# Latent attention in a two-layer trunk: the value product turned round, sums applied behind it, projections between the blocks

## Chip, cores and metric

The kernel runs on one core of one Trainium2 chip. The metric is the device time of the whole launch in microseconds; of the kernel before three runs are known, and their median is the figure that counts.

## What is computed

Two layers of a decoder trunk, 512 tokens of width 1024, float32. Each layer is FFN, token mixer, FFN; every part has a norm ahead and behind, and is scaled, shifted and gated by vectors that come from a conditioning input. Layer 0 mixes by latent attention, layer 1 by a dilated attention. What the change touches is the latent attention and the vectors:

```python
mod = (silu(c) @ w_mod[i] + b_mod[i]).reshape(B, N_SUB, 3, D_MODEL)
...
lat = h @ w_in
cq = lat[..., :Q_LORA]                      # 384
ckv = lat[..., Q_LORA:Q_LORA + KV_LORA]     # 256
k_rope = lat[..., Q_LORA + KV_LORA:]        # 32
q = (rmsnorm(cq, q_norm) @ w_q_up)          # 16 heads of 64 + 32
kv = (rmsnorm(ckv, kv_norm) @ w_kv_up)      # 16 heads of 64 + 64
...
s = einsum('bhqd,bhkd->bhqk', qi, kt) * scale      # causal, blocks of 128 queries
p = softmax(s, axis=-1)
o = einsum('bhqk,bhkd->bhqd', p, vt)
...
return o.reshape(B, S, MLA_HEADS * V_HEAD) @ w_o
```

## The kernel before

The activations lie transposed, 128 partitions by 8 tiles of 512 tokens. Every large product goes as three fp32r passes (`mm3`, L119 to L122): high by high, high by low, low by high. Weights come by DMA on SyncE's queue into a ring of five raw buffers (`load`, L92 to L96), are split into a high part on ScalarE (L103) and a low part on VectorE (L105, two halves), and lie in a ring of six.

The conditioning vectors are made 128 numbers at a time: `mod` loads 512 KB of `w_mod` and multiplies and sums them on VectorE (L128). The vectors that a later part needs wait in the list `todo`; `pump` takes one from it, and `settle` takes what is left for a part before that part needs it. In the first FFN `pump` is called after each head (a gate and up unit) and after each of the first 16 down units; in the attention, after each value product.

A list scheduler sets the order on each engine from the order in which the program is written and from priorities; the copy-out of a finished result has a high one (`HOT`).

The latent attention runs so. Its `head` units make six latents; `norm` scales them (L600, L603, L604), and one of them carries the shared rope key, made by L581 to L583. Then `rest`:

- `values` makes v for all 16 heads, 8 units of six passes, from two normalised latents.
- `keys(g)` makes keys, rope parts and queries of four heads; it is a generator, advanced one piece after every second block while the heads of the group ahead are worked on.
- `attend` takes one head's block of 128 queries: `score` (L671), the causal correction with the row minimum on VectorE (L673), the exponential with the row sum on ScalarE (L676); `turn` transposes the probabilities (L683) and copies them out (L686, L688); `weigh` multiplies them with v (L694), probabilities as the stationary block, and after the fourth block scales each row by the reciprocal of its sum (L703, L707); `close` transposes the result of two heads (L719) and `put_o` splits it into high and low (L550, L551). `Pipe(1)` sets how many steps lie between `score` and `turn`.
- `out_unit` then makes the first three of eight tiles of the output product.

```python
                nc.tensor.matmul(
                    box["o"][:, i * 64 : i * 64 + 64],
                    box[i][:, j * P : (j + 1) * P],
                    self.v[j, h // 8][:, (h % 8) * 64 : (h % 8) * 64 + 64],
```

Of the kernel before, what the change touches and what calls it, by code (L numbers as in the profile page):

```python
# [51 lines left out]
class Trunk:  # L52
    def __init__(self, ctx, tc, a):
        self.ctx, self.tc, self.nc, self.a = ctx, tc, tc.nc, a
        nc = tc.nc
        self.cp = ctx.enter_context(tc.tile_pool(name="const", bufs=1))
        self.ring = ctx.enter_context(tc.tile_pool(name="ring", bufs=SLOTS))
        self.sl = ctx.enter_context(tc.tile_pool(name="sl", bufs=SLICES))
        self.tmp = ctx.enter_context(tc.tile_pool(name="tmp", bufs=2))
        self.ps = ctx.enter_context(tc.tile_pool(name="ps", bufs=4, space=PSUM))  # L60
        self.chunks = {}
# [343 lines left out]
class Ffn:  # L405
# [76 lines left out]
    def rest(self):  # L482
        t = self.t
        for q, (at, n) in enumerate(GROUPS):
# [71 lines left out]
class Mla(Mixer):  # L556
# [53 lines left out]
            t.mm3(b, [x[:, at + j, :] for x in w], self.latn[u], j == 0, j == len(us) - 1)  # L610
        return b

    def values(self):
        t, nc = self.t, self.t.nc
        w = [t.weights(t.a["mla_v"][k], flat=True) for k in range(2)]
        self.v = {}
        for j in range(4):
            for e in range(2):
                b = t.bank()
                for k in range(2):  # L620
                    ls = [x[:, j * P : (j + 1) * P] for x in self.latn[k]]
                    t.mm3(b, ls, [x[:, e * SEQ : (e + 1) * SEQ] for x in w[k]], k == 0, k == 1)
                self.v[j, e] = t.s()
                t.pump(1)
                nc.scalar.activation(self.v[j, e], b, AF.Copy)

    def keys(self, g):
        t, nc = self.t, self.t.nc
        w = []
        q, k = [[t.s() for _ in range(4)] for _ in range(2)]  # L630
        self.qk[g] = q, k

        def pair(p, x, ci, at, us):
            if len(w) <= ci:
                w.append(t.weights(t.a[f"mla_qk{ci}"][g]))
            b = self.project(w[ci], at, us)
            nc.scalar.activation(x[2 * p][0:64], b[0:64], AF.Copy)
            nc.vector.tensor_copy(x[2 * p + 1][0:64], b[64:128])
            if x is k:
                for y in k[2 * p : 2 * p + 2]:  # L640
                    nc.gpsimd.tensor_scalar(y[64:96], self.lat[2][64:96], 1.0, 0.0, ALU.mult, ALU.add)

        def rope():
            b = self.project(w[0], 4, (3, 4, 5))
            t1, t2 = t.t("u", UB), t.t("u", UB)
            nc.vector.stream_shuffle(t2, b, [(c + 16) % 32 for c in range(32)])
            nc.vector.tensor_tensor(t1, b, self.cos, ALU.mult)
            nc.gpsimd.tensor_tensor(t2, t2, self.sin, ALU.mult)
            for j in range(4):
                r = slice(32 * j, 32 * j + 32)  # L650
                nc.vector.tensor_tensor(q[j][64:96], t1[r], t2[r], ALU.add)

        yield pair(0, k, 0, 0, (0, 1))
        yield rope()
        yield pair(0, q, 1, 0, (3, 4, 5))
        yield pair(1, k, 0, 2, (0, 1))
        yield pair(1, q, 1, 3, (3, 4, 5))

    def attend(self, h, q, k, pipe, at):
        t, nc = self.t, self.t.nc  # L660
        sc = 96.0**-0.5
        if at == 0:
            self.st = t.tmp.tile([P, 8], F32, tag="st", name="st", bufs=3), {}
        st, box = self.st
        nm, z = st[:, 0:4], st[:, 4:8]

        def score(i):
            n = (i + 1) * P
            c = slice(i, i + 1)
            s = t.bank()[:, :n]  # L670
            nc.tensor.matmul(s, q[0:96, i * P : n], k[0:96, :n], start=True, stop=True)  # L671
            p = box[i] = t.t("sq", SB)[:, :n]
            nc.vector.tensor_tensor_reduce(  # L673
                p, s, self.mask[:, SEQ - n :], -sc, 3e38, ALU.add, ALU.min, accum_out=nm[:, c]
            )
            nc.scalar.activation(p, p, AF.Exp, bias=nm[:, c], scale=-1.0, accum_out=z[:, c])  # L676

        def turn(i):
            n = (i + 1) * P
            x = t.bank("aux")[:, :n]  # L680
            for j in range(i + 1):
                r = slice(j * P, (j + 1) * P)
                nc.tensor.transpose(x[:, r], box[i][:, r], t.ident)  # L683
            box[i] = t.t("silu" if i % 2 else "gg")[:, :n]
            if i == 3:
                nc.scalar.activation(box[i], x, AF.Copy)  # L686
            else:
                nc.vector.tensor_copy(box[i], x)  # L688

        def weigh(i):  # L690
            if i == 0:
                box["o"] = t.bank("aux")
            for j in range(i + 1):
                nc.tensor.matmul(  # L694
                    box["o"][:, i * 64 : i * 64 + 64],
                    box[i][:, j * P : (j + 1) * P],
                    self.v[j, h // 8][:, (h % 8) * 64 : (h % 8) * 64 + 64],
                    start=j == 0,
                    stop=j == i,
                )  # L700
            if i < 3:
                return
            nc.vector.reciprocal(z, z)  # L703
            if h % 2 == 0:
                self.os = t.t("acc")
            dst = self.os.rearrange("p (i e c) -> p i e c", i=4, e=2)[:, :, h % 2, :]
            nc.vector.tensor_tensor(  # L707
                dst,
                box["o"][:, :256].rearrange("p (i c) -> p i c", i=4),
                z.unsqueeze(2).to_broadcast([P, 4, 64]),  # L710
                ALU.mult,
            )

        def close(i):
            if i == 3 and h % 2:
                x = t.bank("aux")
                for j in range(4):
                    r = slice(j * P, (j + 1) * P)
                    nc.tensor.transpose(x[:, r], self.os[:, r], t.ident)  # L719
                self.put_o(x)  # L720

        pipe.push(at, score, turn, weigh, close)

    def rest(self):
        t = self.t
        self.values()
        self.qk = {}
        pipe = Pipe(1)
        for _ in self.keys(0):
            pass  # L730
        for g in range(4):
            ahead = self.keys(g + 1) if g < 3 else iter(())
            q, k = self.qk[g]
            for j in range(4):
                for i in range(4):
                    self.attend(4 * g + j, q[j], k[j], pipe, i)
                    if (4 * j + i) % KQ == KQ - 1:
                        next(ahead, None)
            for _ in ahead:
                pass  # L740
        pipe.flush()
        for k in range(KT - TAIL):
            self.out_unit(k, 0, SEQ)


class Dil(Mixer):
# [8 lines left out]

    def tables(self):
        t, nc = self.t, self.t.nc
        t.dram = t.ctx.enter_context(t.tc.tile_pool(name="dr", bufs=1, space=bass.MemoryType.DRAM))
# [439 lines left out]
```

## Time and profile before

| what | before |
|---|---|
| median of three runs | 2365.59 us (2364.16 to 2369.31) |
| profiled execution, its own time | 2368.39 us |
| its span, first to last instruction | 2366.2 us |
| mean granted TensorE clock | 0.989 |
| TensorE busy | 2295.6 us, 97% |
| VectorE busy | 1213.2 us, 51% |
| ScalarE busy | 841.8 us, 36% |
| GpSimd busy | 206.4 us, 9% |
| data moved by DMA | 281.5 MB, 119 GB/s on average |

The shares are means over the whole span; the attention is one stage of it, from the first value product at 454.70 us to the last output matmul ahead of the second FFN at 617.40 us. Busy time counts neither register nor DMA-issuing instructions. The matmuls overlap, so that their busy times are longer than the distance between two starts; the granted clock is a share of 2.4 GHz.

### The profile page before, as it was taken

To read this page: it belongs to the slowest core of one execution; us is meant where nothing else is said; L and a number is where in the kernel's file an instruction comes from. 1 tells how busy PE (TensorE), PEld (TensorE's weight loads), DVE (VectorE), ACT (ScalarE), POOL (GpSimd) and SP (SyncE) were. 2 spreads that over 40 slices of the span, in tenths; PEclk is the share of its full clock that TensorE was granted. 3 is DMA by queue.
4 is the path that set the end of the run, shared out by engine and by line. 5 is a ranking of instruction groups with operands and counts; after the bars stand their busy time and mean duration, and the time that the engine had idled before them with its cause. 6 is when DMAs were issued, how large, how long until landed. Compare 5 with 4: busy or idle time off the path is not lost. (4 is left out here: it accounts for less than half of the span.)

```text
span 2366.2 us, 32250 instructions
## 1 busy us (share of the span) xinstructions
PE 2295.6 (97%) x12238; PEld 1936.2 (82%) x12238; DVE 1213.2 (51%) x2748; ACT 841.8 (36%) x1685; POOL 206.4 (9%) x243
## 2 busy tenths in 40 slices
PE   6999999999999999999999999999999999999998
PEld 4888888878888888888888888777777778888887
DVE  7735535688465455376455355444334456423333
ACT  3322224455442222243222243443434345322221
POOL 0000004120230000040000031000000005000002
PEclk9999999999999999999999999999999999999999
DMA  8645431423245454316455313332333322332321
GB/s 304 214 151 175 156 106 63 151 75 95 75 127 185 141 179 149 100 55 207 157 164 167 107 63 114 97 81 81 93 90 86 100 62 64 116 98 89 107 81 36
DMA packets 115135, 281.52 MB, mean 119 GB/s; under 512 B 37905, under 2 KB 44324, under 8 KB 114980
## 3 DMA queue, kind: packets, MB, share of 16 engines
q1 hardware_dynamic: 114980, 279.46, 38.2%
q8 instruction: 96, 1.57, 0.3%
q14 instruction: 59, 0.48, 0.1%
HBM read 277.04 MB, written 2.37 MB: 118 GB/s over the span
## 5 line engine op out<-in xcount | busy, mean ns | idle before, releaser
L120 PE MATMUL mm<-s,whi 128*128 128x512 f32 (+1 forms) x3344 | 1217.8, 366 | 12.9 <-ACT s L550 5.0
L121 PE MATMUL mm<-s,whi 128*128 128x512 f32 (+1 forms) x3344 | 1212.6, 363 | 2.7 <-POOL s L275 1.8
L122 PE MATMUL mm<-s,wlo 128*128 128x512 f32 (+1 forms) x3344 | 1209.9, 363 | 0.0
L103 ACT ACTIVATE whi<-raw 128x1024 fp32r<-128x1024 f32 (+1 forms) x374 | 387.5, 1037 | 1166.7 <-PE mm L121 744.1
L120 PEld LDWEIGHTS mm<-s,whi 128*128 128x128 f32 x3344 | 635.4, 191 | 119.1 <-ACT s L550 5.2
L121 PEld LDWEIGHTS mm<-s,whi 128*128 128x128 f32 x3344 | 636.5, 191 | 98.9 <-POOL s L275 3.6
L122 PEld LDWEIGHTS mm<-s,wlo 128*128 128x128 f32 x3344 | 636.1, 190 | 95.9 <-DVE wlo L105 0.8
L105 DVE TENSOR_TENSOR wlo<-raw,whi 128x512 fp32r<-128x512 f32 (+1 forms) x748 | 489.8, 689 | 419.9 <-ACT whi L103 412.4
L128 DVE CUSTOM_DVE_ANT_0 raw<-raw,cs 128x1024 f32<-128x1024 f32 x128 | 157.0, 1228 | 152.8 <-DMA raw<-w_mod 152.1
L375 POOL TENSOR_TENSOR acc<-acc,sq 128x256 f32<-128x256 f32 (+1 forms) x60 | 57.9, 965 | 1450.0 <-ACT sq L229 1448.9
L449 DVE TENSOR_TENSOR gg<-silu,mm 128x512 f32<-128x512 f32 (+1 forms) x95 | 60.5, 636 | 172.4 <-PE mm L122 170.7
L475 DVE TENSOR_TENSOR s<-mm,s 128x512 f32<-128x512 f32 (+1 forms) x84 | 47.3, 564 | 144.9 <-PE mm L122 144.5
L450 ACT ACTIVATE s<-gg 128x512 fp32r<-128x512 f32 (+1 forms) x97 | 57.4, 591 | 15.4 <-DVE gg L449 13.5
L272 ACT ACTIVATE s<-u,mS 128x256 fp32r<-128x256 f32 (+1 forms) x88 | 42.6, 517 | 56.8 <-DVE u L268 56.8
L853 ACT ACTIVATE s<-mm 128x512 f32<-128x512 f32 (+3 forms) x156 | 46.4, 374 | 32.5 <-PE mm L122 32.5
L229 ACT ACTIVATE sq<-s 128x256 f32<-128x256 f32 (+1 forms) x82 | 36.0, 445 | 60.0 <-DVE s L475 56.9
L953 ACT ACTIVATE u<-u,y 128x128 f32<-128x128 f32 x128 | 49.5, 388 | 15.1 <-DVE y L934 15.1
L452 DVE TENSOR_TENSOR s<-gg,s 128x512 fp32r<-128x512 f32 x79 | 54.2, 686 | 0.3
L447 ACT ACTIVATE silu<-mm 128x512 f32<-128x512 f32 (+1 forms) x95 | 51.4, 541 | 6.7 <-PE mm L122 6.7
L362 DVE TENSOR_TENSOR x<-x,s 128x256 f32<-128x256 f32 x90 | 50.0, 586 | 0.0
L359 DVE SCALAR_TENSOR_TENSOR s<-s,mG,aux 128x256 f32<-128x256 f32 x96 | 41.7, 472 | 14.9 <-PE aux L218 14.9
L249 POOL TENSOR_TENSOR sq<-sq 128x256 f32<-128x256 f32 x50 | 43.5, 870 | 34.3 <-ACT sq L245 32.1
(140 smaller groups left out, 1368.1 us busy)
## 6 DMA issues: line engine op xcount, KB each, us to landing
raw<-w_gu SPq DMA_DIRECT2D x176, 512.0 KB, 3.4
raw<-w_mod SPq DMA_DIRECT2D x128, 512.0 KB, 3.4
raw<-dil_in SPq DMA_DIRECT2D x72, 512.0 KB, 3.4
raw<-w_down SPq DMA_DIRECT2D x64, 448.0 KB, 3.4
raw<-w_down SPq DMA_DIRECT2D x32, 512.0 KB, 3.6
s<-w_mod SPq DMA_DIRECT2D x32, 256.0 KB, 6.6
raw<-mla_o SPq DMA_DIRECT2D x8, 512.0 KB, 3.7
raw<-dil_o SPq DMA_DIRECT2D x8, 512.0 KB, 3.4
```

The costliest lines, as they stand in the source:

```text
L103: self.nc.scalar.activation(hi, raw, AF.Copy)
L105: self.nc.vector.tensor_tensor(lo[:, r], raw[:, r], f(hi[:, r]), ALU.subtract)
L120: mm(out, w[0], m[0], start=first, stop=False)
L121: mm(out, w[0], m[1], start=False, stop=False)
L122: mm(out, w[1], m[0], start=False, stop=last)
L128: nc.vector.tensor_tensor_reduce(raw, raw, self.cs, 1.0, 0.0, ALU.mult, ALU.add, accum_out=t[:, 0:1])
L362: eng.tensor_tensor(self.x[:, k, lo:hi], self.x[:, k, lo:hi], yk, ALU.add)
L375: nc.gpsimd.tensor_tensor(acc, acc, self.sq(yk, n), ALU.add)
L447: nc.scalar.activation(s, banks[0], AF.Silu)
L449: nc.vector.tensor_tensor(v, s, banks[1], ALU.mult)
L450: nc.scalar.activation(ghi, v, AF.Copy)
L452: eng.tensor_tensor(glo, v, f(ghi), ALU.subtract)
```

## The change

- The first FFN takes two vectors after each of its 19 down units, where it took one after 16 of them; what the attention needs is then ready when it begins, and no vector is left for it.
- `weigh` has v as the stationary block, 64 columns wide, and the probabilities moving, 128 columns. The two heads of a pair write partitions 0 to 63 and 64 to 127 of one bank. The result comes out transposed, and the transposes of `close` are gone.
- The reciprocal of the sums is taken once for a pair of heads, stored to a buffer in DRAM and loaded back over 64 partitions per head; a VectorE product (L758) applies it to the finished pair.
- `attend` takes pairs of heads; `Pipe(2)` sets two steps between score and transposes. Only the first key, rope and query pieces come ahead of the blocks; the value, key, rope and query pieces, and part of the first output tile, stand in the table `BESIDE`, by the step after which they are issued. The output product's last eighth of each tile comes at the end.
- Smaller: both copies of a query piece go to ScalarE, the rope sum is one addition with four copies behind it (two on ScalarE, two on GpSimd), the transposed blocks 0 and 1 of both heads are copied at once, and a DRAM pool moves to the constructor.

```diff
             for k in range(KT if q < len(GROUPS) - 1 else KT - TAIL):
                 self.down(q, k, 0, SEQ)
-                if q < len(GROUPS) - 1:
+                if t.first is self:
+                    t.pump(2)
+                elif q < len(GROUPS) - 1:
                     t.pump(1)
...
+    def query(self, g, p):
+        nc = self.t.nc
+        b = self.project(self.weight(g, 1), 3 * p, (3, 4, 5))
+        q = self.q[2 * g + p]
+        for e in range(2):
+            nc.scalar.activation(q[e][0:64], b[64 * e : 64 * e + 64], AF.Copy)
+
+    def rope(self, g):
...
+        nc.vector.stream_shuffle(t2, b, [(c + 16) % 32 for c in range(32)])
+        nc.vector.tensor_tensor(t1, b, self.cos, ALU.mult)
+        nc.gpsimd.tensor_tensor(t2, t2, self.sin, ALU.mult)
+        nc.vector.tensor_tensor(t1, t1, t2, ALU.add)
...
+    BESIDE = {
+        0: (("value", 0, 0), ("key", 0, 1)),
+        1: (("value", 1, 0), ("query", 0, 1)),
...
+        30: (("out_part", 0, 0, SEQ, range(5, 6)),),
+    }
...
         def weigh(i):
             if i == 0:
                 box["o"] = t.bank("aux")
             for j in range(i + 1):
-                nc.tensor.matmul(
-                    box["o"][:, i * 64 : i * 64 + 64],
-                    box[i][:, j * P : (j + 1) * P],
-                    self.v[j, h // 8][:, (h % 8) * 64 : (h % 8) * 64 + 64],
-                    start=j == 0,
-                    stop=j == i,
-                )
-            if i < 3:
-                return
-            nc.vector.reciprocal(z, z)
...
-        def close(i):
-            if i == 3 and h % 2:
-                x = t.bank("aux")
-                for j in range(4):
-                    r = slice(j * P, (j + 1) * P)
-                    nc.tensor.transpose(x[:, r], self.os[:, r], t.ident)
-                self.put_o(x)
-
-        pipe.push(at, score, turn, weigh, close)
+                for e in range(2):
+                    h = 2 * c + e
+                    nc.tensor.matmul(
+                        box["o"][64 * e : 64 * e + 64, i * P : (i + 1) * P],
+                        self.v[j, h // 8][:, (h % 8) * 64 : (h % 8) * 64 + 64],
+                        box[i][e][:, j * P : (j + 1) * P],
+                        start=i == j == 0,
+                        stop=i == j == 3,
+                        skip_group_check=True,
+                    )
+            if i == 3:
+                r = box["r"]
+                nc.vector.tensor_tensor(r, box["o"], r, ALU.mult)
+                self.put_o(r)
+
+        pipe.push(i, score, turn, weigh)
+
+    def sums(self, st):
+        t, nc = self.t, self.t.nc
+        d0 = t.dram.tile([2, SEQ], F32, tag="d0", name="d0", bufs=2)
+        z = st[:, :, 2:4]
+        nc.vector.reciprocal(z, z)
+        r = t.t("acc")
+        for e in range(2):
+            nc.sync.dma_start(d0[e : e + 1].rearrange("e (i p) -> p i e", p=P), z[:, :, e : e + 1])
+            nc.sync.dma_start(r[64 * e : 64 * e + 64], d0[e : e + 1].broadcast_to([64, SEQ]))
+        return r
 
     def rest(self):
-        t = self.t
-        self.values()
...
+        self.wv, self.wqk, self.v, self.q, self.k = [], {}, {}, {}, {}
+        pipe = Pipe(2)
+        self.key(0, 0)
+        self.rope(0)
+        self.query(0, 0)
+        for c in range(8):
+            for i in range(4):
+                self.attend(c, i, pipe)
+                for name, *args in self.BESIDE.get(4 * c + i, ()):
+                    getattr(self, name)(*args)
+        ks = range(KT - TAIL)
+        for k in ks:
+            pipe.step()
+            self.out_part(k, 0, SEQ, range(0 if k else 6, KT - 1))
         pipe.flush()
-        for k in range(KT - TAIL):
-            self.out_unit(k, 0, SEQ)
+        for k in ks:
+            self.out_part(k, 0, SEQ, range(KT - 1, KT))
```

How the instructions lie now is seen at three places. In the changed kernel lines up to the FFN have numbers one higher, those of the attention some three or more.

TensorE, at the end of the latent projections and the start of the attention proper, before (L195 sums the squares of a latent, L218 spreads the norm's factor; `whi,s` is a value pass):

```order
L122 MATMUL mm<-s,wlo 128x256
L195 MATMUL aux<-ones,sq 128x1 x4
L120 MATMUL mm<-whi,s 128x512
L121 MATMUL mm<-wlo,s 128x512
L122 MATMUL mm<-whi,s 128x512
...
L195 MATMUL aux<-ones,sq 128x1 x2
...
L218 MATMUL aux<-ident,rs 128x128 x2
```

And the same place now (L196 and L219 are the same two lines; `s,whi` is a key, rope or query pass):

```order
L196 MATMUL aux<-ones,sq 128x1 x4
L121 MATMUL mm<-s,whi 128x512
L122 MATMUL mm<-s,whi 128x512
L123 MATMUL mm<-s,wlo 128x512
...
L196 MATMUL aux<-ones,sq 128x1 x2
L219 MATMUL aux<-ident,rs 128x128 x2
L121 MATMUL mm<-s,whi 128x512 x2
L122 MATMUL mm<-s,whi 128x512
```

Before, value passes stood behind the sums and on both sides of the spread factor; now six key passes stand between, and behind the factor the rope and query passes, which read the latents that it scales.

VectorE, in the latent projections around the rope key, before (L128 is a vector):

```order
L600 SCALAR_TENSOR_TENSOR u<-s,small,aux 128x256 x2
L581 TENSOR_TENSOR u<-mm,s 32x256
L128 ISA raw,mt<-raw,cs 128x1024
L128 ISA mt 128x1
L604 TENSOR_TENSOR s<-u,s 128x256
L582 TENSOR_TENSOR u<-mm,s 32x256
L604 TENSOR_TENSOR s<-u,s 128x256
L583 TENSOR_TENSOR s<-u 32x256
```

and now:

```order
L603 SCALAR_TENSOR_TENSOR u<-s,small,aux 128x256 x2
L584 TENSOR_TENSOR u<-mm,s 32x256
L607 TENSOR_TENSOR s<-u,s 128x256
L585 TENSOR_TENSOR u<-mm,s 32x256
L607 TENSOR_TENSOR s<-u,s 128x256
L586 TENSOR_TENSOR s<-u 32x256
```

The vector between the two rope products is gone from this place.

SyncE's queue in the attention, now (`d_` is the DRAM buffer of a pair, `st` its sums, `acc` what is loaded back):

```order
L96 DMA raw<-mla_qk 128x768
L96 DMA raw<-mla_o 128x1024 x3
L770 DMA d_4015<-st 128x4x1 x2
L771 DMA acc<-d_4015 64x512 x2
L770 DMA d_4199<-st 128x4x1 x2
L771 DMA acc<-d_4199 64x512 x2
L96 DMA raw<-mla_o 128x1024 x2
L770 DMA d_4354<-st 128x4x1 x2
L771 DMA acc<-d_4354 64x512 x2
```

On VectorE, the product that waits for one of these loads now stands so (L712 is the causal correction, L736 a copy of transposed probabilities, L554 the low part of the result):

```order
L712 ISA sq,st<-mm,s 128x384
L712 ISA st 128x1
L736 COPY silu<-aux 128x256
L758 TENSOR_TENSOR acc<-aux,acc 128x512
L554 TENSOR_TENSOR s<-acc,s 128x512
L712 ISA u,st<-mm,s 128x512
L712 ISA st 128x1
```

Each pair adds four DMAs to the queue between weight loads, and the corrections of the next pair's last score stand behind the product.

## Rows read from the trace of the kernel before

**Rows 1.** Windows of the latent attention; columns: stretch, length, busy PE PEld DVE ACT POOL, PEclk, DMA.

```profile
454.70:617.40 162.70, 158.75 (x927) 128.68 (x927) 125.74 (x352) 82.75 (x199) 22.38 (x22) 0.99 0.31 98
```

**Rows 2.** Timeline of TensorE in that stretch; start us, length us, instruction, count.

```profile
500.31 1.00 PE L694 MATMUL aux<-s,silu 128*128 128x64 f32 x8
501.12 0.48 PE L120 MATMUL mm<-s,whi 128*128 128x512 f32 x1
501.44 0.39 PE L121 MATMUL mm<-s,whi 128*128 128x512 f32 x1
...
506.49 0.60 PE L683 MATMUL aux<-ident,sq 128*128 128x128 f32 x4
506.93 0.78 PE L694 MATMUL aux<-s,gg 128*128 128x64 f32 x6
```

**Rows 3.** Timeline of TensorE in the dilated layer.

```profile
1596.27 1.09 PE L1027 MATMUL aux<-silu,s 128*64 128x128 f32 x16
1597.29 0.50 PE L120 MATMUL mm<-s,whi 128*128 128x512 f32 x1
1597.63 0.39 PE L121 MATMUL mm<-s,whi 128*128 128x512 f32 x1
1597.86 0.40 PE L122 MATMUL mm<-s,wlo 128*128 128x512 f32 x1
```

**Rows 4.** Windows of the attention, line L694 alone; columns as in rows 1, the instructions in brackets.

```profile
454.70:617.40 162.70, 43.13 (x320) 42.14 (x320) 0.99 0.31 98
```

**Rows 5.** Timeline of the latent norm, TensorE and ScalarE.

```profile
453.89 0.95 PE L195 MATMUL aux<-ones,sq 128*128 128x1 f32 x8
...
459.96 1.02 ACT L603 ACTIVATE s<-u 128x256 fp32r<-128x256 f32 x3
```

**Rows 6.** VectorE's groups in the attention; count | busy us, mean ns | idle before, releaser.

```profile
L128 DVE CUSTOM_DVE_ANT_0 raw<-raw,cs 128x1024 f32<-128x1024 f32 x14 | 17.0, 1217 | 0.0
...
L673 DVE CUSTOM_DVE_ANT_0 sq<-mm,s 128x512 f32<-128x512 f32 x16 | 10.9, 684 | 1.6 <-PE mm L671 1.0 <-PE aux L683 0.5
...
L646 DVE STREAM_SHUFFLE u<-mm 128x512 f32<-128x512 f32 x4 | 2.9, 730 | 0.0
```

**Rows 7.** GpSimd's group there.

```profile
L648 POOL TENSOR_TENSOR u<-u,s 128x512 f32<-128x512 f32 x4 | 5.1, 1278 | 78.1 <-DVE u L646 78.1
```

**Rows 8.** Timeline of VectorE and TensorE in the latent projections.

```profile
425.32 1.28 DVE L128 CUSTOM_DVE_ANT_0 raw<-raw,cs 128x1024 f32<-128x1024 f32 x1
...
427.55 0.36 PE L120 MATMUL mm<-s,whi 128*128 128x256 f32 x1 [2.50 <-DVE u L582]
```

**Rows 9.** TensorE's waits in the attention: total us, times, longest us.

```profile
PE aux L683 <- ACT sq L676: 1.3, 3, 0.9
PE mm L671 <- DVE s L638: 1.2, 1, 1.2
PE mm L120 <- DVE s L638: 0.6, 1, 0.6
```

**Rows 10.** Windows around two waits; columns as in rows 1.

```profile
428.00:438.00 10.00, 10.00 (x48) 9.76 (x47) 4.98 (x14) 2.03 (x4) 1.68 (x1) 0.50 0.60 201
478.00:484.00 6.00, 5.44 (x16) 3.52 (x16) 4.56 (x13) 2.93 (x7) 0.00 (x0) 0.72 0.43 128
```

**Rows 11.** Windows in the first FFN; columns as in rows 1.

```profile
30.00:50.00 20.00, 18.46 (x78) 14.14 (x78) 19.23 (x52) 4.59 (x8) 0.00 (x0) 1.00 1.03 388
90.00:120.00 30.00, 30.00 (x134) 24.86 (x133) 20.21 (x41) 8.76 (x12) 0.00 (x0) 1.00 0.73 234
```

**Rows 12.** ScalarE's groups in the attention.

```profile
L676 ACT ACTIVATION_READ_ACCUMULATOR sq<-sq,st 128x1 f32 x64 | 12.0, 188 | 0.0
L676 ACT ACTIVATE sq<-sq,st 128x512 f32<-128x512 f32 x16 | 11.5, 717 | 6.2 <-DVE st L673 6.2
```

**Rows 13.** Line L918, stores of sums in the dilated layer, 512 pieces of 8 bytes.

```profile
DMA to landing us min/median/max: 3.3/4.5/6.0
```

**Rows 14.** Line L980, broadcast loads of 128 KB in the dilated layer.

```profile
DMA to landing us min/median/max: 2.8/3.1/3.5
```

More of the change, by code (lines that the diff above doesn't have):

```diff
@@ L611, in project @@
         return b
-    def values(self):
-        t, nc = self.t, self.t.nc
-        w = [t.weights(t.a["mla_v"][k], flat=True) for k in range(2)]
-        self.v = {}
-        for j in range(4):
-            for e in range(2):
[L619 to L657, printed above, removed]
@@ L659, in attend, with value, weight @@
-    def attend(self, h, q, k, pipe, at):
+    def value(self, j, e):
+        t = self.t
+        if not self.wv:
+            self.wv += [t.weights(t.a["mla_v"][k], flat=True) for k in range(2)]
+        b = t.bank()
+        for k in range(2):
+            ls = [x[:, j * P : (j + 1) * P] for x in self.latn[k]]
+            t.mm3(b, ls, [x[:, e * SEQ : (e + 1) * SEQ] for x in self.wv[k]], k == 0, k == 1)
+        self.v[j, e] = t.s()
+        t.nc.scalar.activation(self.v[j, e], b, AF.Copy)
+    def weight(self, g, ci):
+        t = self.t
+        if (g, ci) not in self.wqk:
+            self.wqk[g, ci] = t.weights(t.a[f"mla_qk{ci}"][g])
+        return self.wqk[g, ci]
@@ new lines, in key @@
+    def key(self, g, p):
+        t, nc = self.t, self.t.nc
+        b = self.project(self.weight(g, 0), 2 * p, (0, 1))
+        k = self.k[2 * g + p] = [t.s() for _ in range(2)]
+        nc.scalar.activation(k[0][0:64], b[0:64], AF.Copy)
+        nc.vector.tensor_copy(k[1][0:64], b[64:128])
+        for y in k:
+            nc.gpsimd.tensor_scalar(y[64:96], self.lat[2][64:96], 1.0, 0.0, ALU.mult, ALU.add)
+    def query(self, g, p):
[4 more added lines that the diff above has]
+            nc.scalar.activation(q[e][0:64], b[64 * e : 64 * e + 64], AF.Copy)
@@ new lines, in rope @@
+    def rope(self, g):
+        t, nc = self.t, self.t.nc
+        b = self.project(self.weight(g, 0), 4, (3, 4, 5))
+        t1, t2 = t.s(), t.s()
+        nc.vector.stream_shuffle(t2, b, [(c + 16) % 32 for c in range(32)])
+        nc.vector.tensor_tensor(t1, b, self.cos, ALU.mult)
+        nc.gpsimd.tensor_tensor(t2, t2, self.sin, ALU.mult)
+        nc.vector.tensor_tensor(t1, t1, t2, ALU.add)
+        for p in range(2):
+            q = self.q[2 * g + p] = [t.s() for _ in range(2)]
+            for e in range(2):
+                r = t1[64 * p + 32 * e : 64 * p + 32 * e + 32]
+                if p:
+                    nc.gpsimd.tensor_scalar(q[e][64:96], r, 1.0, 0.0, ALU.mult, ALU.add)
+                else:
+                    nc.scalar.activation(q[e][64:96], r, AF.Copy)
@@ new lines @@
+    BESIDE = {
+        0: (("value", 0, 0), ("key", 0, 1)),
+        1: (("value", 1, 0), ("query", 0, 1)),
+        2: (("value", 2, 0),),
+        3: (("value", 3, 0),),
+        4: (("key", 1, 0),),
+        5: (("rope", 1),),
+        6: (("query", 1, 0),),
+        7: (("value", 0, 1),),
+        8: (("key", 1, 1),),
+        9: (("query", 1, 1),),
+        10: (("value", 1, 1),),
+        11: (("value", 2, 1),),
+        12: (("key", 2, 0),),
+        13: (("rope", 2),),
+        14: (("query", 2, 0),),
+        15: (("value", 3, 1),),
+        16: (("key", 2, 1),),
+        17: (("query", 2, 1),),
+        19: (("key", 3, 0),),
+        20: (("rope", 3),),
+        21: (("query", 3, 0),),
+        23: (("key", 3, 1),),
+        24: (("query", 3, 1),),
+        28: (("out_part", 0, 0, SEQ, range(0, 3)),),
+        29: (("out_part", 0, 0, SEQ, range(3, 5)),),
+        30: (("out_part", 0, 0, SEQ, range(5, 6)),),
+    }
@@ L678, in turn @@
         def turn(i):
             n = (i + 1) * P
-            x = t.bank("aux")[:, :n]
-            for j in range(i + 1):
-                r = slice(j * P, (j + 1) * P)
[L683 to L686, printed above, removed]
-            else:
-                nc.vector.tensor_copy(box[i], x)
+            tag = "gg" if i % 2 else "silu"
+            ps = [t.bank("aux")]
@@ new lines, in turn @@
+            ys = [t.t(tag)]
+            if i < 2:
+                ps.append(ps[0][:, n:])
+                ys.append(ys[0][:, n:])
+            else:
+                ps.append(t.bank("aux"))
+                ys.append(t.t(tag))
+            for e in range(2):
+                for j in range(i + 1):
+                    r = slice(j * P, (j + 1) * P)
+                    nc.tensor.transpose(ps[e][:, r], box[i][e][:, r], t.ident)
+            if i < 2:
+                nc.vector.tensor_copy(ys[0][:, : 2 * n], ps[0][:, : 2 * n])
+            else:
+                nc.scalar.activation(ys[0][:, :n], ps[0][:, :n], AF.Copy)
+                nc.vector.tensor_copy(ys[1][:, :n], ps[1][:, :n])
@@ L690, in weigh @@
+            box[i] = ys
         def weigh(i):
@@ L722, in attend @@
-        pipe.push(at, score, turn, weigh, close)
-    def rest(self):
-        t = self.t
-        self.values()
[L727 to L740, printed above, removed]
+                for e in range(2):
+                    h = 2 * c + e
[6 more added lines that the diff above has]
+                        skip_group_check=True,
+                    )
@@ new lines, in weigh @@
+            if i == 3:
+                r = box["r"]
[3 more added lines that the diff above has]
+    def sums(self, st):
+        t, nc = self.t, self.t.nc
+        d0 = t.dram.tile([2, SEQ], F32, tag="d0", name="d0", bufs=2)
+        z = st[:, :, 2:4]
+        nc.vector.reciprocal(z, z)
+        r = t.t("acc")
+        for e in range(2):
+            nc.sync.dma_start(d0[e : e + 1].rearrange("e (i p) -> p i e", p=P), z[:, :, e : e + 1])
+            nc.sync.dma_start(r[64 * e : 64 * e + 64], d0[e : e + 1].broadcast_to([64, SEQ]))
+        return r
```

38 lines of the change are left out of this document (15 added, 23 removed).

## Prediction

> **What bounds the kernel now.** I read the cores view first, then the windows of the latent attention, then TensorE's groups and its timeline there, then the waits. From the first value product to the last matmul ahead of the next FFN, TensorE is busy 158.8 of 162.7 us while VectorE is busy 125.7 [rows 1]: TensorE sets the end, and VectorE is near enough to hold it now and then. So a matmul saved here is time saved, and a wait of TensorE is time lost at its full length. A busy time of TensorE overlaps with its neighbours', so I price its instructions from start to start: eight L694 matmuls run from 500.31 to the next start at 501.12, 0.101 us each; four transposes L683 from 506.49 to 506.93, 0.11 each [rows 2]; a 512-column pass of a three-pass product 0.23 [rows 3].
>
> **The weighing.** Before, 320 instructions L694 [rows 4] have the probabilities as stationary block and 64 columns of v moving: 320 x 0.101 = 32.3 us. Now v is stationary, 128 columns move, and the two heads of a pair lie on the two column halves; the count stays 320. The kernel does just this in its dilated layer: sixteen L1027 matmuls from 1596.27 to 1597.29, 0.064 each [rows 3]. So 320 x 0.064 = 20.5 us, a gain of 11.8. Bounds: if the halves overlapped wholly, half a 128-column transpose, 0.055 each, a gain of 14.7; if they did not overlap, 0.11 each [rows 2], a loss of 2.9. I take the middle value because the row is the same shape.
>
> **The transposes of the result** (L719, 8 pairs x 4) go: 32 x 0.11 = 3.5 us. No bound needed.
>
> **The start of the attention.** Before, 48 value passes stood behind the last latent's norm and hid it; now only the first key's six do (the order above). The last head's sums of squares are through at 453.89, the normalised latents are written from 459.96 to 460.98 [rows 5], the first of them at about 460.3, so some 6.0 us lie between them; six passes cover 6 x 0.23 = 1.4. TensorE stands 4.6 us. Then the rope product: shuffle 0.73 [rows 6], GpSimd's product 1.28 [rows 7], an addition and a copy of some 0.7 and 0.6 (estimates from rows of like size), start-up some 0.3, in all 3.6, beside nine query passes (2.0): another 1.6 to 2.8, I take 2.0. After an idle stretch the trace shows TensorE's clock at half: after the 2.50 us wait at 427.55 [rows 8] it stood at 0.50 (1.2 of 2.4 GHz) from 428 to 438, which costs 10 x 0.5 = 5.0 us; around waits of 1.2 and 0.6 us near 478 [rows 9] it was 0.72 on average from 478 to 484, 6 x 0.28 = 1.7 us [rows 10]. For idle of 6.6 us I take 5.0. What stood there before goes: waits 1.2 and 0.6, clock 1.7, in all 3.5. Net +6.6 + 5.0 - 3.5 = +8.1; bounds +2.3 (no second idle, 1.7 for the clock, -0.5 for passes that slip in) and +10.5 (2.8 idle and a second dip).
>
> **The vectors.** 22 of 56 vectors (512 KB load, L128 1.22 us [rows 6] and three small operations) move from the attention to the first FFN, 14 of them from the stage of rows 1. In the latent projections one, at 425.32 for 1.28 us, stood on VectorE between the two rope products of the key latent; TensorE waited 2.50 us there [rows 8]. That wait falls to about 1.2. What clock follows an idle of 1.2 I take from the nearest row, 478 to 484, so 1.7 instead of 5.0. Gain 1.3 + 3.3 = 4.6; bounds 1.3 (the dip stays) and 6.3 (it goes). In the first FFN each of 19 down units takes two vectors now: 1.5 MB in some 4.9 us is 310 GB/s, against 234 GB/s now at 90 to 120 us and 388 reached at 30 to 50 us [rows 11]. VectorE has two vectors (3.0 with the small operations), two halves of a weight (1.3) and an addition (0.7), so 5.0 us in a unit of TensorE's 4.8; six weights in the ring cover the difference for part of each run of eight units. Cost +1.0, bounds 0 and 4.
>
> **The deeper lag.** A block's transposes followed its score by one step of one head; now by two steps of a pair, with projections between. The waits of L683 on the exponentials, 1.3 us [rows 9], go. -1.3, bounds -3 and +6 (below).
>
> **The sums through memory.** 1/z now goes out in two stores and back in two broadcasts per pair, and VectorE's product L758 waits for it with the next pair's score corrections behind it. From the end of the last score: two corrections of 0.68 [rows 6], the first half over by then, an exponential 0.72 with its read of 0.19 [rows 12], and some 0.3 for small operations (an estimate): 2.2 us. Issue 0.4, the store 4.5 (3.3 to 6.0 for 512 pieces of 8 bytes) [rows 13], issue 0.5, the broadcast 3.1 [rows 14]: 10.7 us. TensorE's work from that score to the pair's last weighing is 21 passes (pairs 0 to 3), six scores (1.3), 20 transposes (2.2) and 40 weighing instructions (2.6): 10.9 us; for pairs 5 and 6, with 15 passes, 9.5. So the sums come up to 1.2 us late. VectorE may be late by about one step (a quarter of a pair's 14 us, 3.5) before TensorE wants a bank that the held corrections occupy. Cost 0.
>
> **The sum** goes against the profiled execution's own 2368.4 us: -11.8 - 3.5 + 8.1 - 4.6 + 1.0 - 1.3 = -12.1, hence 2356.3. That execution is 2.8 us over the median of the runs, so **2353.5 us** on their basis. A measurement can tell about 0.2% (4.7 us) from no change.
>
> **A rule against it.** After a group of L1027 the first pass takes 0.34 to the next start, 0.11 more than the second's 0.23 [rows 3]; after L694, which uses the whole width, it takes 0.32 [rows 2]. Leaving the halves costs 0.02 more than leaving the old form, and entering them lies in the 0.064. The Trainium skill, "TensorEngine Tiling (Array Packing)", Tiling Modes, Key Properties, says that changing the tiling mode drains TensorE. By that rule each of 32 weighing groups would empty the engine twice; the trace agrees only as far as those 0.02 us. Without it the sum stands as above, with it see the third rival.
>
> **The rivals.**
> 1. *More is gained*, 2346: the second product of the keys or the scores fill the start and no dip follows the shortened wait (start +2.3 for +8.1, projections -6.3 for -4.6: 7.5 less). For it: the dip near 478 cost a third of the one from 428 on [rows 10]. Against: the order has no work to fill the 4.6 us. Chance 0.14.
> 2. *Late sums*, slower, 2378: the 4-byte pieces of two stores queue behind each other and land after 11 us rather than 4.5. The chain is then 17.2 us, some 7 over TensorE's work and 3.6 over the one step of slack; seven pairs (the last has output work behind it) lose 25 us. It decides from a chain of about 16 us on, where the gain is gone. For it: twice as many pieces as in the row, in two stores at once. Against: L918 never took over 6.0. Chance 0.07.
> 3. *The halves cost a drain*, no change, 2364: a switch empties the engine, in and out. A 512-column pass lasts 0.39 and its successor starts after 0.23 [rows 3], so a drain is 0.16; 32 x 2 x 0.16 = 10.2 us more. Against: 0.064 and 0.02 above. Chance 0.06. Beyond it, halves that do not overlap: 2353.5 + 14.7 = 2368.
> 4. *The steps wait on each other*, 2361: score, correction, exponential, transpose, copy now run in pairs, so four banks are full after two scores and a projection; 1 us per pair on top, 8 in all. For it: VectorE is busy for about 12 of each pair's 14 us by my count. Against: the lag of two steps. Chance 0.17.
>
> **How the numbers follow.** The forecast has 0.56, its own range 2347 to 2360. Faster by over 0.2% (below 2360.9) are the forecast, the first rival and half of the fourth: 0.79. Slower are the late sums and a corner of the FFN's bound: 0.07. The rest, 0.14, is within 0.2%. The range, 2342 to 2365, leaves out the late sums, the halves without overlap and the far end of the first rival.
>
> **What would show it.** Right: L748 starts 0.06 to 0.07 us apart; TensorE idle 4 to 5 us on the latent norm right after the projections and about 2 on the rope; clock near 0.5 for some 10 us behind them; stage from the first key to the last output product some 10 us shorter; no w_mod load in the attention; the store of d0 landing in 4 to 5 us. Wrong: VectorE idle on L758 for several us per pair with TensorE idle behind it; a first FFN over 4 us longer; L748 at 0.1.

## The result, and the profile after

The changed kernel takes 2377.61 us in the median (2376.53 to 2379.57, four runs) against 2365.15 for the kernel before: ratio 1.005, 95% interval 1.0033 to 1.0068. It is slower by 12.5 us where 12 us less were forecast. The profiled execution took 2376.53 us.

The page of the changed kernel, its first lines:

```profile
span 2374.7 us, 32197 instructions
...
PE 2293.0 (97%) x12206; PEld 1922.3 (81%) x12206; DVE 1196.7 (50%) x2696; ACT 849.8 (36%) x1701; POOL 205.3 (9%) x251
```

TensorE has 32 instructions less, as the diff says, and a little less work. What it lost is idle time and clock, and both lie in the attention. Its windows (columns as in rows 1; the stage now runs from 449.02 to 620.57):

```profile
449.02:475.00 25.98, 21.24 (x85) 15.74 (x85) 12.24 (x33) 14.63 (x32) 5.66 (x8) 0.93 0.19 56
475.00:543.00 68.00, 67.59 (x425) 49.52 (x424) 39.97 (x113) 42.47 (x102) 10.41 (x14) 1.00 0.16 39
543.00:620.57 77.57, 66.80 (x387) 48.68 (x386) 34.97 (x94) 31.63 (x79) 3.74 (x5) 0.90 0.21 56
449.02:620.57 171.55, 155.62 (x894) 113.94 (x894) 87.17 (x239) 88.72 (x213) 19.81 (x27) 0.95 0.18 49
```

The stage has grown from 162.70 us [rows 1] to 171.55. It begins 5.7 us earlier, so the projections ahead gained; the middle is full; the last 77 us are not, with 10.8 us of idle and a mean clock of 0.90. TensorE's waits in the stage (total, times, longest), where [rows 9] stood before:

```profile
PE aux L734 <- DVE acc L758: 3.2, 1, 3.2
PE aux L748 <- DVE gg L736: 3.1, 3, 1.3
PE mm L709 <- DVE st L712: 2.4, 1, 2.4
PE mm L121 <- ACT s L553: 1.8, 1, 1.8
PE mm L709 <- ACT s L664: 1.8, 1, 1.8
PE aux L219 <- POOL rs L216: 1.2, 1, 1.2
PE mm L121 <- ACT s L606: 1.0, 1, 1.0
PE mm L709 <- ACT s L647: 0.8, 1, 0.8
```

The last four are the start, 4.8 us. The first four, 10.5 us, name four different instructions, but the same thing stands ahead of each in the timeline. VectorE's waits begin with this row:

```profile
DVE acc L758 <- DMA acc<-d: 32.0, 8, 11.5
```

Eight times, once per pair, VectorE stands still at the product with 1/z until the broadcast load has landed, 32.0 us in all. The two transfers on its way, line L770 (the stores) and line L771 (the loads), with the time from the issue until the data are there (the landing):

```profile
DMA to landing us min/median/max: 7.9/8.5/8.9
```

```profile
DMA to landing us min/median/max: 2.8/4.1/4.8
```

The rows that answer to them before are [rows 13] and [rows 14], 4.5 and 3.1 us. One such wait in the timeline of all engines:

```profile
574.72 1.98 PE L709 MATMUL mm<-s 96*128 96x512 f32 x4
...
575.02 1.31 SPq L771 DMA_DIRECT2D acc<-d  x2
...
578.00 0.49 PE L734 MATMUL aux<-ident,sq 128*128 128x128 f32 x3
580.80 0.69 DVE L758 TENSOR_TENSOR acc<-aux,acc 128x512 f32<-128x512 f32 x1 [6.32 <-DMA acc<-d]
581.41 0.68 DVE L712 CUSTOM_DVE_ANT_0 u<-mm,s 128x512 f32<-128x512 f32 x1
...
581.64 0.87 PE L734 MATMUL aux<-ident,sq 128*128 128x128 f32 x3 [3.16 <-DVE acc L758]
...
584.67 0.93 SPq L770 DMA_DIRECT2D d<-st  x2
```

The load is issued at 575.02, VectorE waits 6.32 us for it with the next pair's correction L712 behind, and TensorE, in the middle of a group of six transposes, stands 3.16 us until VectorE moves again. The lateness is also handed on. The next pair's last scores (L709) are through at 576.71, but their corrections stand behind the wait, so that pair's own store goes out at 584.67, 8.0 us behind its scores. From the end of a pair's last scores to its L758 the first pair takes 14.9 us, the second 15.8, the fifth 21.4 and the seventh 20.9; TensorE's stops begin behind the fourth pair's product (544.32).

Behind three of the four stops the clock is low; behind the one of 1.3 us at 602 it stays at 1.00. The windows of 10 us around the stops at 546, 581 and 617 us:

```profile
545.00:555.00 10.00, 8.03 (x33) 6.37 (x34) 6.46 (x20) 3.99 (x11) 0.73 (x1) 0.66 0.45 157
575.00:585.00 10.00, 5.64 (x31) 3.42 (x30) 3.97 (x13) 2.86 (x8) 0.00 (x0) 0.83 0.43 131
585.00:595.00 10.00, 10.00 (x60) 7.57 (x58) 3.14 (x11) 2.85 (x12) 0.00 (x0) 0.83 0.05 0
615.00:625.00 10.00, 7.89 (x41) 6.65 (x40) 3.97 (x6) 6.13 (x11) 2.61 (x2) 0.83 0.15 55
```

The clock's loss there is what lacks to 1.00, times the length: (0.34 + 0.17 + 0.17 + 0.17) x 10 = 8.5 us. With the 10.5 of idle that makes 19.0 us. The last window reaches past the stage's end at 620.57; by the row from 543 on the stage itself lost some 7.8 us (0.10 x 77.57), so that 18.3 of the 19.0 lie in it.

### The profile page after: what moved, and what is told of

The parts are those of the page before. It is cut to its first block, busy times and chain, and to the rows that moved or that the text cites. A ratio compares the mean times of both kernels' runs of the same rounds, so it can differ in the third digit from the quotient of the medians.

```text
span 2374.7 us, 32197 instructions
## 1 busy us (share of the span) xinstructions
PE 2293.0 (97%) x12206; PEld 1922.3 (81%) x12206; DVE 1196.7 (50%) x2696; ACT 849.8 (36%) x1701; POOL 205.3 (9%) x251
```

## The experiments

**Is it the sums?** The theory: the late sums hold VectorE in order, VectorE holds TensorE, and the clock falls behind it. The rival: the steps wait on each other. `free_sums` takes the way through memory out:

```diff
-        for e in range(2):
-            nc.sync.dma_start(d0[e : e + 1].rearrange("e (i p) -> p i e", p=P), z[:, :, e : e + 1])
-            nc.sync.dma_start(r[64 * e : 64 * e + 64], d0[e : e + 1].broadcast_to([64, SEQ]))
-        return r
+        return t.t("acc")
...
-                nc.vector.tensor_tensor(r, box["o"], r, ALU.mult)
+                nc.vector.tensor_tensor(r, box["o"], self.cos, ALU.mult)
```

> The changed kernel without the way of the sums through memory: the stores and loads of 1/z are left out and the finished pair is multiplied by a table that lies ready, so the scaling by 1/z is not made. Theory (the late sums hold TensorE): the idle of TensorE behind L758, 10.8 us, and the half clock behind it, 8.5 us, go; about 2358 us. Rival (the steps wait on each other and the halves cost their switches): at most a third of that goes, 2371 us or more.

Measured 2355.91 us, ratio to before 0.9962 (0.9943 to 0.9981). The attention took 152.6 us (in the profiled execution, at 2345.78 us the fastest of seven), 18.9 less than in the changed kernel, where the sum above gave 18.3 to 19.0. That they lie so close is partly luck, since two profiles of the changed kernel differ by 2.9 us in this stage (below); but of TensorE's waits only the four of the start are left. The rival falls.

**Why is the store slow?** `row_sums` turns the eight columns of sums into eight rows first:

```diff
+        z = t.tmp.tile([P, 8], F32, tag="rz", name="rz", bufs=2)
+        nc.vector.reciprocal(z.rearrange("p (e i) -> p i e", e=2), st[:, :, 2:4])
+        x = t.bank("aux")[0:8, 0:P]
+        nc.tensor.transpose(x, z, t.ident)
+        zt = t.tmp.tile([8, P], F32, tag="zt", name="zt", bufs=1)
+        nc.vector.tensor_copy(zt, x)
+        nc.sync.dma_start(d0.rearrange("e (i p) -> (e i) p", p=P), zt)
```

> The changed kernel with 1/z of a pair turned by one TensorE transpose into 8 rows, stored as 8 pieces of 512 bytes in place of 1024 pieces of 4. Theory (the many small pieces make the store slow): the store lands in 3 to 4.5 us in place of 8.5, the wait at L758 falls under 1 us per pair, about 2360 us. Rival (a store to memory and a load behind it are slow whatever the pieces): the store stays at 7 us or more, and the time at 2374 us or more.

Measured 2356.95 us, ratio 0.9967 (0.9955 to 0.998): faster than both kernels. VectorE no longer waits for a DMA at L758. From the store's issue to the loads' it is 1.2 to 3.2 us now, 1.3 in the median (timeline of SyncE's queue), and the attention takes 155.2 us:

```profile
481.74 0.34 SPq L772 DMA_DIRECT2D d<-zt  x1
482.99 1.15 SPq L775 DMA_DIRECT2D acc<-d  x2
```

```profile
451.55:606.75 155.20, 150.22 (x903) 110.61 (x902) 89.45 (x246) 88.24 (x211) 19.96 (x27) 0.98 0.16 54
```

Is it the number of pieces, their size, or the one queue? `two_queues` issues the second store from ScalarE:

```diff
-            nc.sync.dma_start(d0[e : e + 1].rearrange("e (i p) -> p i e", p=P), z[:, :, e : e + 1])
+            q = nc.scalar if e else nc.sync
+            q.dma_start(d0[e : e + 1].rearrange("e (i p) -> p i e", p=P), z[:, :, e : e + 1])
```

> The changed kernel with the second of a pair's two stores of 1/z issued from ScalarE's queue in place of SyncE's. Theory (1024 pieces of 4 bytes take the DMA engines their time, whoever issues them): both land after some 8 us, 2377 us. Rival (the second store waits behind the first in one queue, so each alone takes 4.5 us as L918 did): they land after 4.5 us, the waits at L758 go, 2360 us.

Measured 2378.04 us, ratio 1.0047 (1.0029 to 1.0065), the store's landing (min, median, max):

```profile
DMA to landing us min/median/max: 8.0/8.1/9.1
```

The queue is not the cause. Nor is it the moving of the pieces as the trace records it. The stores of the second pair are issued at 494.74 and the loads that wait for them at 502.82; the changed kernel's windows in between (columns as in rows 1, DMA share next to last):

```profile
494.70:496.60 1.90, 1.90 (x19) 1.55 (x19) 1.09 (x6) 1.85 (x6) 0.00 (x0) 1.00 0.27 2
496.60:502.60 6.00, 6.00 (x39) 4.88 (x38) 3.23 (x8) 3.03 (x8) 0.00 (x0) 1.00 0.00 0
```

All packets of the two stores lie in the first 1.9 us; then the DMA engines have none for 6 us, and still the data count as landed only after them. What passes in this time no run shows.

`short_rows` keeps small pieces but makes them fewer, as the sums lie:

```diff
+        z = t.tmp.tile([P, 8], F32, tag="rz", name="rz", bufs=2)
+        nc.vector.reciprocal(z.rearrange("p (e i) -> p i e", e=2), st[:, :, 2:4])
+        nc.sync.dma_start(d0.rearrange("e (p r) -> (e p) r", r=8), z)
```

> The changed kernel with 1/z of a pair stored as it lies, 128 pieces of 32 bytes in one store, and loaded back by the same loads; the factors come back in another order, so each token gets the reciprocal of another's sum. Theory (the number of pieces sets the landing: 8.3 us for 1024, 1.9 for 8): some 2.6 us, the attention within 2 us of row_sums' 155.2, 2357 us. Rival (pieces under 512 bytes are slow each by themselves): the landing stays over 5 us and VectorE waits at L758, 2368 us or more.

Measured 2358.15 us, ratio 0.9969 (0.9947 to 0.9991), the attention 152.5 us, and the store:

```profile
DMA to landing us min/median/max: 1.4/1.4/1.4
```

128 pieces of 32 bytes land in 1.4 us, two stores of 512 pieces of 4 bytes in 8.5: (8.5 - 1.4) / (1024 - 128) = 0.0079 us per piece. By it one store of 512 pieces takes 1.4 + 384 x 0.0079 = 4.4 us; the dilated layer's took 4.5 [rows 13]. Another store of that layer, L977 in the kernel before, has 256 pieces of 16 bytes: the rule gives 2.4 and it took 2.3 in the median. So the time follows the number of pieces. All these ways store 4 KB, so that more pieces are always smaller ones; that the size alone would do nothing is not shown, only that a piece of 4, 8 or 16 bytes more costs about the same.

**More time for the sums.** `close_later` puts L758 and the splitting into a stage of their own, a step behind:

```diff
-            if i == 3:
+        def close(i):
+            if i == 3:
                 r = box["r"]
...
-        pipe.push(i, score, turn, weigh)
+        pipe.push(i, score, turn, weigh, close)
```

> The changed kernel with L758 and the splitting behind it one step later, a bank held longer. Theory (VectorE blocked in order by the late sums): one step is 3.5 to 4 us, the waits at L758 were 4.0 each, so they fall under 1 us; about 2362 us. Rival (the steps wait on each other): no change, 2374 to 2380 us.

Measured 2374.76 us, ratio 1.004 (1.0024 to 1.0055). The time is the rival's, but it says nothing on the theory: the scheduler put L758 at the same place on VectorE, between the third block's corrections and the fourth's, and it waited there 31.0 us. Moving the call in the program did not move the instruction.

**The start.** `values_ahead` moves four value units and the second key ahead of the blocks:

```diff
         self.key(0, 0)
+        for j in range(4):
+            self.value(j, 0)
         self.rope(0)
         self.query(0, 0)
+        self.key(0, 1)
...
-        0: (("value", 0, 0), ("key", 0, 1)),
-        1: (("value", 1, 0), ("query", 0, 1)),
-        2: (("value", 2, 0),),
-        3: (("value", 3, 0),),
+        1: (("query", 0, 1),),
```

> The changed kernel with the first four value units and the second key ahead of the blocks, between the first key and the rope and behind the query. Theory (the start costs 4.7 us of idle and 1.7 us of clock): 6 us less, 2371 us. Rival (the cover that the sums had beside the first pairs is gone, so that they hold TensorE there): no gain, 2376 us or more.

Measured 2374.3 us, ratio 1.0037 (1.0025 to 1.005), between the two: the late sums still kept VectorE 30.8 us at the product. `rows_ahead` is this edit and that of `row_sums` together:

> row_sums with values_ahead: the sums in 8 rows, and four value units and the second key ahead of the blocks. Theory (with the sums in time, the start's idle of 4.7 us and its clock of 1.7 us are what is left): 6 us under row_sums, 2351 us. Rival (the start's clock follows the projections, not this idle, or the first pairs lose their cover): 2355 us or more.

Measured **2349.83 us** (2345.68 to 2353.16), ratio 0.9939 (0.9923 to 0.9955): the fastest version, and 7.1 us under `row_sums`. Its attention is 148.7 us long, nearly all of it busy and at full clock:

```profile
452.45:601.12 148.67, 146.85 (x902) 108.15 (x902) 89.22 (x246) 87.32 (x211) 19.92 (x27) 1.00 0.18 57
```

**The halves.** In the changed kernel's timeline of TensorE the groups of transposes and of weighing have a length that is not proportional to their number:

```profile
477.94 0.82 PE L734 MATMUL aux<-ident,sq 128*128 128x128 f32 x6
478.69 0.66 PE L748 MATMUL aux<-gg,s 128*64 128x128 f32 x8
479.28 0.50 PE L121 MATMUL mm<-s,whi 128*128 128x512 f32 x1
...
482.61 0.88 PE L748 MATMUL aux<-silu,s 128*64 128x128 f32 x12
483.42 0.50 PE L121 MATMUL mm<-s,whi 128*128 128x512 f32 x1
```

Eight weighing instructions take 479.28 - 478.69 = 0.59 us, twelve 0.81, and sixteen (from 487.20 to 488.22) 1.02: 0.0547 for each and 0.15 on top of a group. Six transposes ahead of a weighing take 0.75, not 6 x 0.109 = 0.65: 0.10 on top. The 0.0547 is a mean: in the trace's starts the two heads' instructions begin 6 to 7 ns apart, and the next two 0.109 us later, so the halves run side by side. Of the 0.15, 0.05 stands behind the first two instructions and 0.10 behind the last. `full_width` is `row_sums` with the stationary block 128 columns wide:

```diff
-                        box["o"][64 * e : 64 * e + 64, i * P : (i + 1) * P],
-                        self.v[j, h // 8][:, (h % 8) * 64 : (h % 8) * 64 + 64],
+                        box["o"][:, i * P : (i + 1) * P],
+                        self.v[j, h // 8][:, (2 * c % 8) * 64 : (2 * c % 8) * 64 + 128],
...
-                        start=i == j == 0,
-                        stop=i == j == 3,
+                        start=i == j == e == 0,
+                        stop=i == j == 3 and e == 1,
```

> row_sums with the weighing on all 128 columns: the stationary block is v of both heads, both heads' probabilities move over it and add up in one bank, so each head's result holds the other's product too. Theory (32 changes to column halves and back cost 0.095 and 0.15 us each): the transposes fall from 0.130 to 0.109 us each (3.1 us less), a weighing instruction takes 0.109 us with nothing on top per group (34.9 in place of 22.3 us); 9.5 us over row_sums, 2366 us. Rival (no cost of a change; the 0.15 belongs to the first matmul behind any new weights): transposes stay at 0.130, 2370 us or more.

Measured 2364.05 us, ratio to before 0.9994 (0.9983 to 1.0005), 7.1 us over `row_sums`. The same place in its timeline:

```profile
477.39 0.82 PE L734 MATMUL aux<-ident,sq 128*128 128x128 f32 x6
478.04 1.06 PE L748 MATMUL aux<-gg,s 128*128 128x128 f32 x8
478.85 0.48 PE L122 MATMUL mm<-s,whi 128*128 128x512 f32 x1
```

Six transposes take 0.65 us again and eight weighing instructions 0.81, so 0.10 each. The additions belong to the halves, as they go with them: 0.10 + 0.15 = 0.25 us for each of 32 groups, 8 us in all. The halves are still worth it, by the 7.1 us.

**The vectors.** `one_vector` undoes the first FFN's part in the changed kernel, `vectors_alone` adds it alone to the kernel before:

```diff
-                if t.first is self:
-                    t.pump(2)
-                elif q < len(GROUPS) - 1:
+                if q < len(GROUPS) - 1:
                     t.pump(1)
```

> The changed kernel with the first FFN's rule of before: 16 down units with one vector each, 22 vectors left for the projections. Theory: the wait and the half clock in the projections come back, 2377.6 + 6 = 2383 us. Rival: no difference, 2377 us.

Measured 2396.57 us, ratio 1.0133 (1.0112 to 1.0154): 19 us over the changed kernel, three times what the theory said, and not for its reason. No vector came back to the projections, and the wait there stayed as short as in the changed kernel:

```profile
423.73 0.36 PE L121 MATMUL mm<-s,whi 128*128 128x256 f32 x1 [1.35 <-ACT sq L230]
```

The 22 vectors fall into the new attention, between 510 and 616 us, with the late sums still in it; the stage is 20 us longer than in the changed kernel (waits of TensorE, then VectorE's group):

```profile
PE mm L707 <- DVE mt L132: 3.4, 1, 3.4
...
PE aux L732 <- DVE mt L132: 3.0, 1, 3.0
```

```profile
L129 DVE CUSTOM_DVE_ANT_0 raw<-raw,cs 128x1024 f32<-128x1024 f32 x22 | 26.8, 1217 | 8.3 <-DMA raw<-w_mod 8.3
```

> The kernel before with the first FFN's two vectors per down unit alone. Theory (the vectors' part of the change gains by itself): the 2.5 us wait in the latent projections shrinks and the half clock behind it goes, the first FFN stays within 1 us; 5 to 6 us less than before, 2359 us. Rival (the vectors cost in the first FFN what they give): 2365 us.

Measured 2369.84 us, ratio 1.0019 (1.0007 to 1.0031), not the 6 us less of the theory. The value products of the kernel before still take one vector each, now those of the next part, and the scheduler puts one into the old place:

```profile
422.96 1.28 DVE L128 CUSTOM_DVE_ANT_0 raw<-raw,cs 128x1024 f32<-128x1024 f32 x1
```

```profile
PE mm L120 <- DVE u L584: 2.5, 1, 2.5
```

So the wait of [rows 8] stayed. It went in the changed kernel because its value products take no vector, and not through the first FFN: in `one_vector` it is gone without the first FFN's part, here it stands with it. Why this version is slower than before by 0.2% rather than equal, its profile does not say.

**Two profiles of one kernel.** Between the attention's end and the kernel's, the first profile of the change loses another 5 us on instructions that are the same as before and in the same order.

> The changed kernel once more, unaltered, for a second profile and more times. The stretches outside the attention have the same instructions in the same order as before; theory (the 5 us between the attention's end and the kernel's that the first profile shows more come from where the clock dips fall, which is not the change's): another division of them between the transitions, the attention's length within 1 us of 171.6. Rival (a lasting effect of the change): the same three steps of 1.5 us at 670, 1040 and 1990 us.

> The kernel before once more, unaltered, for a second profile. Theory (clock dips differ from run to run): the attention within 1 us of 162.7 us, the rest apart by some us in the transitions between the parts. Rival: the same to 1 us everywhere.

Measured 2379.56 us, ratio 1.0052 (1.0038 to 1.0067), and 2366.56 us, ratio 0.9997 (0.9983 to 1.001). The attention took 174.4 us in the second profile of the change, not within 1 us of the first, and 161.2 in that of the kernel before, 1.5 less than in its first, so both theories missed on the attention's length. Two stretches of the kernel before, in its first profile and then in its second:

```profile
1980.00:2000.00 20.00, 17.21 (x136) 16.12 (x134) 14.77 (x32) 12.40 (x28) 10.90 (x13) 1.00 0.25 83
660.00:680.00 20.00, 18.15 (x127) 17.66 (x126) 14.43 (x33) 9.85 (x24) 7.59 (x9) 0.83 0.17 54
```

```profile
1980.00:2000.00 20.00, 18.04 (x123) 17.56 (x123) 13.28 (x29) 9.68 (x24) 8.80 (x12) 0.83 0.24 80
660.00:680.00 20.00, 16.75 (x134) 16.14 (x135) 12.55 (x29) 9.03 (x22) 9.27 (x11) 1.00 0.25 81
```

The clock fell at 660 in one execution and at 1980 in the other, 0.17 x 20 = 3.4 us each. Short waits between the parts are followed by a fall in some executions and not in others, and a difference of a few us between two single profiles there is not the change's. The rival of a lasting effect falls: the second profile of the change gained 3 us between 671 and 1025 us on the first.

## Why the prediction was wrong

The step that failed is the one on the sums through memory, with its "Cost 0". The mechanism was looked for at the right place, on VectorE's order at L758, but two terms of the chain were too small. The store was priced at 4.5 us and took 8.5, the load at 3.1 and took 4.1; with them the prediction's chain is 15.7 us, not 10.7. Against its 9.5 to 10.9 us of TensorE's work that is 5 to 6 late, past the 3.5 of slack. The store's price was taken from a row with 512 pieces, the kernel has 1024 at once, and the text itself said "twice as many pieces as in the row". The third term was the 2.2 us ahead of the store: it holds for the first two pairs (1.9 and 2.5), and then each wait holds up the next pair's corrections, so that it grew to as much as 8.0. The prediction saw the corrections behind the product, but did not count what that does to the next pair's sums.

The second rival, late sums at 2378 us with a chance of 0.07, is what happened. It asked for a store of 11 us and lost 25 us in idle alone; 8.5 was enough, because the lateness is handed on, and because the clock fell behind three of the four stops (10.5 idle, 8.5 clock). That its time came out within 1 us is luck: it took no account of the clock, the drain or the milder start.

Point by point:

- *Weighing*, 11.8 less: right that the halves gain, wrong in how. Summed from start to start over the stage, L694 took 32.2 us, L748 22.3 in `row_sums`, where the clock was low only at the start: 9.9 less. The middle value 0.064 is no partial overlap: the halves overlap wholly, which was the bound with 0.055 and a gain of 14.7, and a price per group comes on top. The row of sixteen hid the 0.15, which weighs more on groups of four and eight.
- *The drain* (third rival, 10.2 us, chance 0.06): its cost exists, 0.25 us per group, 8 us, of which the 0.064 held some 3. The argument against it looked only at the way out of the halves; the way in was charged to the transposes, which the prediction never priced anew (16.9 us before, 20.8 in `row_sums`). The Trainium skill, "TensorEngine Tiling (Array Packing)", Tiling Modes, Key Properties, says that a change of the tiling mode drains the engine; the runs agree in that the change costs time, 0.25 us for a group.
- *Transposes of the result*, 3.5 less: right, L719's 32 instructions and their time are gone.
- *The start*, +8.1: too dear. Idle was 4.8 us rather than 6.6, and the clock lost 1.8 us (0.93 from 449.02 to 475.00), not 5.0: some +3.1. `rows_ahead` against `row_sums` gives 6.5 us of the stage.
- *Vectors*: the projections gained 5.7 us by the stage's start, where 4.6 was forecast; the wait at the rope key is 1.36 us now (timeline of TensorE, first line below) and no clock fell behind it. Much of this is luck. In `before_again` the kernel before has the same wait of 2.50 us, and the clock behind it is 1.00 (second line), where it was 0.50 in the first profile [rows 10]: some 5 us that the prediction booked as lost before, and partly as won now, come in one execution and not in another. And the wait did not shrink through the first FFN (`one_vector`, `vectors_alone`). The first FFN ends 0.2 us later, not 1.0.

```profile
426.34 0.35 PE L121 MATMUL mm<-s,whi 128*128 128x256 f32 x1 [1.36 <-ACT sq L230]
```

```profile
428.00:438.00 10.00, 9.10 (x77) 8.90 (x76) 7.86 (x19) 4.61 (x9) 1.68 (x1) 1.00 0.61 191
```

- *The deeper lag*: right, the wait of the transposes on the exponentials is gone. The fourth rival, 8 us for steps that wait on each other, is not seen: with the sums out of the way (`free_sums`) no wait of TensorE is left in the stage behind its start.

The stage was to fall by 11.8 + 3.5 + 1.3 - 8.1 = 8.5 us; it grew by 8.9. The gap of 17.4 is the late sums (+18.9 by `free_sums`), the drain beyond what the 0.064 held (some +5) and the start (-5.0). These make 18.9, 1.5 us too much, which is within what two profiles of one kernel differ by in this stage.

## What to carry to other kernels

For a small round trip through memory, count the pieces that it is stored in: here the same 4 KB took 1.4 us in 128 pieces and 8.5 in 1024. Put a small table into rows (one transpose) before it is stored. VectorE works in order, so a wait for such a transfer stops whatever stands behind it, the next round trip's beginning too; TensorE can then pay twice, once idle and once in clock. A fall of the clock behind one wait in one profile is no fixed price: here it came and went between executions of the same kernel. Parts of one change have to be timed together and apart: the vectors in the first FFN are worth 19 us with the new attention and no gain with the old, and with the sums and the start mended the same change is 0.6% faster than the kernel before.

## What was not expected of the hardware

- A store's landing time followed 1.4 us + 0.0079 us for each piece beyond 128, for 4 KB in pieces of 4, 8, 16 and 32 bytes, and most of it passed while the trace has no packet of the store any more (6 of 8 us for 1024 pieces). The Trainium skill, "DMA: Bandwidth & Descriptors", Specifications, gives 512 bytes as the least size for full rate; no run here measures a rate, but 128 pieces of 32 bytes landed in 1.4 us.
- Issuing half of the pieces from a second queue changed nothing (8.1 us).
- Matmuls of 128 columns on the two column halves start 6 to 7 ns apart, two every 0.109 us, the time of one on the full width; going into the halves and back costs 0.25 us for a group.
- The same wait of 2.50 us was followed by 10 us at half the clock in one execution of the kernel before, and by none in another.
